# Products on half of the array in a two-layer network: one half after the other, or alternating

## The chip, the core and the metric

The program runs on one NeuronCore of a Trainium2 chip. The metric is the device time of one execution in microseconds (us). One execution was also recorded by the hardware profiler; all rows below come from that one. TensorE (PE) multiplies a stationary operand, which a weight load (PEld) puts into its array of 128 rows by 128 columns, with a moving operand, and writes into PSUM banks. VectorE (DVE), ScalarE (ACT) and GpSimd (POOL) do the rest; SyncE (SP) issues the DMAs.

## The reference, cut to what matters

A sequence of 512 positions with 1024 channels passes an even layer, an odd layer and a hybrid layer. Each has feed-forward parts, which take most of the time and which the change leaves alone. The mixers hold what the change touches, all of it in f32:

- Even layer, S5 branch: 32 groups of 16 channels, each with 64 complex states. The output of a group is what its own inputs give within blocks of eight positions, plus the real and the imaginary part of the state at the block's start, each times a matrix.
- Even layer, SSD branch (Mamba-2): eight heads of 64 channels in four pairs. A head's output is a masked product inside each chunk (`y_diag`) plus a product with the state carried in (`y_off`).
- Odd layer: attention with eight heads of 64 channels. `scores = q k^T / 8 + bias`, a softmax over the causal band, and the product with `v`.
- Hybrid layer: three attentions, plain and dilated, with eight heads of 64 channels each, combined by their softmax denominators; beside them a convolution of 31 taps and gates.

## The kernel before

Channels lie on the 128 partitions, so two heads of 64 channels, or the states of two S5 groups, lie in one tile: the first in partitions 0 to 63, the second in 64 to 127. A product over the 64 channels of one head uses only one half of the array's rows; a product whose result has 64 channels uses one half of its columns. The program's own operations go through small helpers, so all matmuls show as line L294 and all transposes as L297; the operands' names tell them apart. The large projections hold f32 values as a sum of two rounded parts (`xh` and `xl`, `wh` and `wl`) and make three products; the small products named here are plain f32 matmuls, which the trace shows as two instructions each.

A scheduler orders the instructions of each engine by priorities and a simulated clock. Where the code is inside `self.pe_order()`, TensorE's instructions keep the order in which the code emits them; work from outside such a region may still come between.

**S5** (`even`, the loop over `gh` and `gq`). Each quarter `gq` loads `tq` (cleared by POOL, then eight DMAs) and `cq` (two DMAs) into the tag `par`, which has three buffers. For each of its eight groups `g` it makes three products into one accumulator: `tq` with `ug` (all 128 rows), then `cq` with `hr` and `cq` with `hi` (64 rows, half `g2`). The two halves write into two banks, `pv[0]` and `pv[1]`. These products are not in a fixed order.

**SSD** (`ssd`, `out_y` and `out_o`), inside a fixed order: for head `s` of the pair all chunks `c`, then for the other head. The results of the two heads lie in different partitions of one bank, so each uses one half of the array's columns.

**Odd attention** (`odd`), inside a fixed order. There are 32 units, one for each pair of heads `j`, head `s` and block `qt` of 128 queries, in that order. `score` makes one product of 64 rows with N = 128 (qt + 1) keys (`qk` tiles, `qn` in the trace) into a bank `aux`; VectorE adds the bias `bt` and takes the maximum, ScalarE makes the exponentials `p`. `turn` transposes `p` on TensorE and copies it out (`pT`), `values` multiplies with `vt`. The loop over units is a pipeline written by hand:

```python
turn(u)
if n:
    values(units[n - 1])
...
if n + 2 < 32:
    score(units[n + 2])
for _ in range(share[j][n % 8]):
    next(plan[j], None)
```

so a unit's score stands two units ahead of its transposes, and `plan` fills in steps of the next pair's projections and other work. The bias `bt` of a head is loaded by SP when the head's first score is emitted (two buffers), and POOL then overwrites a corner of it.

**Hybrid attention** (`hybrid` and the class `AttnState`), with the same pipeline: 32 units of pair `j`, `kind` (plain, or the two dilated ones), head `s` and half `up` of the sequence. A score makes two products (plain) or four (dilated) from the tiles `r`. `filler` puts in projections and, for each of its steps, convolution taps on VectorE; from unit 22 on the projections of its first list are used up, and a new list starts at unit 26.

There are eight PSUM banks: three `mm`, three `aux`, two `acc`.

Of the kernel before, what the change touches and what calls it, by code (L numbers as in the profile page):

```python
# [17 lines left out]
T = 512  # L18
# [233 lines left out]
class Net:  # L252
# [721 lines left out]
    def even(self, gain):  # L974
# [110 lines left out]
        for gh in range(2):  # L1085
            pv = [self.psum("aux").rearrange("p (g c) -> p g c", g=8) for _ in range(2)]
            for gq in (2 * gh, 2 * gh + 1):
                tq = q.tile([128, 8, 128], F32, name="par", tag="par", bufs=3)

                nc.gpsimd.memset(tq, 0.0)  # L1090
                for s in range(8):
                    nc.sync.dma_start(tq[16 * s:16 * s + 16, :, 16 * s:128], self.d_kt[:, 8 * gq:8 * gq + 8, 0:128 - 16 * s])
                cq = q.tile([128, 2, 4, 128], F32, name="par", tag="par", bufs=3)
                for ri in range(2):
                    nc.sync.dma_start(cq[:, ri], self.d_cp[ri, :, 4 * gq:4 * gq + 4])
                for g in range(8):
                    j, g2 = g // 2, g % 2
                    s = slice(64 * g2, 64 * g2 + 64)
                    o = pv[g2][:, 4 * (gq % 2) + j]
                    self.mm(o, tq[:, g], ug[:, 8 * gq + g], True, False)  # L1100
                    self.mm(o, cq[s, 0, j], hr[s, 4 * gq + j], False, False)
                    self.mm(o, cq[s, 1, j], hi[s, 4 * gq + j], False, True)
            ysb = q.tile([128, 16, 64], F32, name="ysb", tag="ysb", bufs=1)
            for g2 in range(2):
                self.act(ysb[:, g2:16:2], pv[g2], AF.Copy)
            for t in range(8):
                nc.sync.dma_start(dy[256 * gh:256 * gh + 256, t].rearrange("(g i) c -> i g c", i=16), ysb[16 * t:16 * t + 16])
# [180 lines left out]
    def ssd(self, q, xs, bc, ya):  # L1288
# [50 lines left out]
        def out_y(j):  # L1339
            psY = psYs[j] = self.psum("acc")  # L1340
            xdt, mts = xdts[j], mtss[j]
            for s in range(2):
                hs = slice(64 * s, 64 * s + 64)
                for c in range(4):
                    self.mm(psY[hs, C(c)], xdt[:, 128 * c + 64 * s:128 * c + 64 * s + 64], mts[s][:, C(c)], True, True)

        def out_o(j):
            g = j // 2
            psO, psY = self.psum("acc"), psYs[j]
            hst, ea = hsts[j], eas[j]  # L1350
            for s in range(2):
                hs = slice(64 * s, 64 * s + 64)
                for c in range(1, 4):
                    o = 128 * (c - 1) + 64 * s
                    self.mm(psO[hs, C(c)], hst[:, o:o + 64], bc[:, 2 + g, C(c)], True, True)
            y = ya[j]
            self.stt(y, xs[:, j], self.vec("ssd_d", j), psY, ALU.mult, ALU.add)
            self.mul(ea[:, 128:], ea[:, 128:], psO[:, 128:])
            self.add(y[:, 128:], y[:, 128:], ea[:, 128:], self.on("ea") if j < 3 else None)
# [4 lines left out]
    def odd(self, gain):  # L1364
# [101 lines left out]
        Wo = self.stream(A["od_out"][0], 4)  # L1466
        fill = out0(Wo)

        def score(u):
            j, s, qt = u["j"], u["s"], u["qt"]  # L1470
            q = qa
            qk = args[j][0]
            if qt == 0:
                bt = q.tile([128, T], F32, name="bt", tag="bt", bufs=2)
                nc.sync.dma_start(bt, A["relb"][2 * j + s])
                nc.gpsimd.memset(bt[0:64, 448:512], NEG)
                self.bt = bt
                if s == 0:
                    args[j].append(q.tile([128, 4, 2], F32, name="st", tag="st", bufs=2))
            hs = slice(64 * s, 64 * s + 64)  # L1480
            N = 128 * (qt + 1)
            ps = self.psum("aux")
            self.mm(ps[:, 0:N], qk[0][hs, C(qt)], qk[1][hs, 0:N], True, True)
            p = u["p"] = q.tile([128, T], F32, name="p", tag="p", bufs=3)
            m = q.tile([128, 2], F32, name="m", tag="m", bufs=4)
            nc.vector.tensor_tensor_reduce(out=p[:, 0:N], in0=ps[:, 0:N], in1=self.bt[:, T - N:], scale=1.0, scalar=NEG,
                                           op0=ALU.add, op1=ALU.max, accum_out=m[:, 0:1])
            self.ts(m[:, 1:2], m[:, 0:1], -1.0, None, ALU.mult)
            self.act(p[:, 0:N], p[:, 0:N], AF.Exp, bias=m[:, 1:2], accum_out=args[j][2][:, qt, s:s + 1])

        def turn(u):
            qt = u["qt"]
# [43 lines left out]
        OP = ['0000010001202', '00000001111020020020', '0011000002000200002', '001010010003003000133']  # L1536
        for _ in mix(*[((pr[0], po[0], po[1])[int(c)], 1) for c in OP[0]], (pr[0], ALL), (po[0], ALL)):
            pass
        units = [dict(j=j, s=s, qt=qt) for j in range(4) for s in range(2) for qt in range(4)]
        plan = [mix(*[((pr[n + 1], po[n + 1], po[n + 2] if n < 2 else None, fill)[int(c)], 1) for c in OP[n + 1]],  # L1540
                    (pr[n + 1], ALL), (po[n + 1], ALL)) for n in range(3)] + [fill]
        share = [[1, 2, 3, 1, 3, 0, 1, 9], [2, 2, 2, 2, 3, 0, 1, 9], [2, 2, 2, 3, 1, 3, 1, 9], [1, 1, 1, 0, 0, 1, 0, 0]]
        next(plan[0])
        score(units[0])
        score(units[1])
        next(plan[0])
        for n, u in enumerate(units):
            j = u["j"]
            turn(u)
            if n:  # L1550
                values(units[n - 1])
            if n % 8 == 2 and n > 8:
                finish(j - 1)
            if n + 2 < 32:
                score(units[n + 2])
            for _ in range(share[j][n % 8]):
                next(plan[j], None)
        values(units[31])
# [15 lines left out]
    def hybrid(self):  # L1574
# [87 lines left out]
        order = self.pe_order()  # L1662
        order.__enter__()
        at8 = AttnState(self, q, rots, vts, oo, oT)
        units = [dict(j=j, kind=kind, s=s, up=up) for j in range(4) for kind in range(2) for s in range(2) for up in range(2)]

        def early():
            for s in HY_STEPS[:HY_STEPS.index("g0")]:
# [20 lines left out]

        filler(LEAD)  # L1690

        at8.score(units[0])
        at8.score(units[1])
        for n, u in enumerate(units):
            if n == SW:
                filler(99)
                for _ in taps:
                    pass
                side.close()
                gp = side.enter_context(tc.tile_pool(name="hyg", bufs=1, side="right", reuse_waits="tile"))  # L1700
                fill = late()
            k = SHARE[n]
            at8.turn(u)
            filler(k // 2)
            at8.values(u)
            if n % 8 == 2 and n > 8:
                at8.finish(u["j"] - 1)
            if n + 2 < 32:
                at8.score(units[n + 2])
            filler(k - k // 2)  # L1710
        for _ in fill:
            pass
# [335 lines left out]
class AttnState:  # L2048
# [5 lines left out]
        self.net, self.nc, self.q, self.rots, self.vts, self.oo = net, net.nc, q, rots, vts, oo  # L2054
        self.st, self.ps, self.oT = {}, {}, oT

    def score(self, u):
        net, nc, q = self.net, self.nc, self.q
        j, kind, s, up = u["j"], u["kind"], u["s"], u["up"]
        C = lambda c: slice(128 * c, 128 * c + 128)  # L2060
        if s == 0 and up == 0:
            self.st[j, kind] = q.tile([128, 4, 2, 2], F32, name=f"st{kind}", tag=f"st{kind}", bufs=2)
        st = self.st[j, kind]
        mask = net.cst("mask12" if kind else "mask0")
        hs = slice(64 * s, 64 * s + 64)
        ps = net.psum("aux")
        p = u["p"] = q.tile([128, T], F32, name="p", tag="p", bufs=3)
        ng = q.tile([128, 2], F32, name="ng", tag="ng", bufs=4)
        lo = u["lo"] = [0, 0]
        for uu in range(2):  # L2070
            t = 2 * up + uu
            b = 256 * uu
            if kind == 0:
                r = self.rots[j, 0]
                lo[uu] = 128 if t == 0 else 0
                k0 = 128 * (t - 1) + lo[uu]
                net.mm(ps[:, b + lo[uu]:b + 256], r[hs, 0, C(t)], r[hs, 1, k0:128 * t + 128], True, True)
            else:
                for i in range(2):
                    r = self.rots[j, 1 + i]  # L2080
                    net.mm(ps[:, b + 128 * i:b + 128 * i + 128], r[hs, 0, C(t)], r[hs, 1, C(t)], True, True)
        for uu in range(2):
            t = 2 * up + uu
            sl = slice(256 * uu + lo[uu], 256 * uu + 256)
            nc.vector.tensor_tensor_reduce(
                out=p[:, sl], in0=ps[:, sl], in1=mask[:, lo[uu]:256],
                scale=1.0, scalar=NEG, op0=ALU.add, op1=ALU.max, accum_out=st[:, t, s, 0:1])
        net.ts(ng, st[:, 2 * up:2 * up + 2, s, 0], -1.0, None, ALU.mult, eng=net.on("ng"))
        for uu in range(2):
            t = 2 * up + uu  # L2090
            sl = slice(256 * uu + lo[uu], 256 * uu + 256)
            net.act(p[:, sl], p[:, sl], AF.Exp, bias=ng[:, uu:uu + 1], accum_out=st[:, t, s, 1:2])

    def turn(self, u):
        net, nc = self.net, self.nc
# [90 lines left out]
```

## Time and profile before

| what | value |
|---|---|
| median of 3 runs | 2797.98 us (2795.88 to 2798.4) |
| the profiled execution's own time | 2793.72 us |
| its span, first to last instruction | 2791.9 us |
| mean granted TensorE clock | 0.981 |
| TensorE busy | 2718.7 us (97%) |
| VectorE, ScalarE, GpSimd busy | 67%, 57%, 32% |

TensorE's busy time is no measure of how fast it works: matmuls are pipelined, and the ends drawn are modelled, so an instruction can be drawn past the start of the next. The distance from one start to the next is what an instruction costs. [...]

### The profile page before, as it was taken

What the parts mean: (1) busy time and instruction counts of PE and PEld (TensorE: products, weight loads), DVE (VectorE), ACT (ScalarE), POOL (GpSimd) and SP (SyncE); (2) the same over time, 40 slices, a digit from 0 to 9 for tenths busy, and PEclk for the clock granted to TensorE, in tenths of its full rate; (3) what the DMA queues carried; (4) which work ended last, traced back from release to release, by engine and by line L of the source; (5) the groups of instructions that cost most, each with busy time, mean ns of one, the idle gap of its engine ahead of it and who ended that gap; (6) DMA issues with size and microseconds to landing.
All of it is one profiled execution on the core that took longest, in us unless ns stands there. A gap on an engine that the chain in (4) does not pass through costs nothing. (4 is left out here: it accounts for less than half of the span.)

```text
span 2791.9 us, 43952 instructions
## 1 busy us (share of the span) xinstructions
PE 2718.7 (97%) x16616; PEld 2410.2 (86%) x16616; DVE 1862.9 (67%) x3368; ACT 1581.1 (57%) x2525; POOL 893.8 (32%) x793
## 2 busy tenths in 40 slices
PE   8899999998999999999999999999999999999997
PEld 6798987878999999998777899988888788989997
DVE  7786756577576885866556758675786534666664
ACT  5366743646576776766334657663443443466674
POOL 5752513224344353342001433421000101345252
PEclk9999998999999999999999999999999899999998
DMA  5433346222332323324221233234333223233321
GB/s 181 120 105 106 95 159 128 82 71 69 103 114 99 106 87 108 113 92 127 69 72 63 67 109 108 98 114 143 92 90 94 68 90 107 69 91 105 115 88 57
DMA packets 106180, 277.44 MB, mean 99 GB/s; under 512 B 31920, under 2 KB 34608, under 8 KB 105968
## 3 DMA queue, kind: packets, MB, share of 16 engines
q1 hardware_dynamic: 105824, 274.44, 31.3%
q8 instruction: 131, 2.15, 0.3%
q14 instruction: 81, 0.66, 0.1%
q10 hardware_dynamic: 144, 0.18, 0.0%
HBM read 256.44 MB, written 11.85 MB: 96 GB/s over the span
## 5 line engine op out<-in xcount | busy, mean ns | idle before, releaser
L291 ACT ACTIVATE wh<-raw 128x1024 fp32r<-128x1024 f32 (+2 forms) x467 | 443.5, 954 | 610.8 <-PE mm L294 448.3
L294 PE MATMUL mm<-xh,wh 128*128 128x512 f32 (+1 forms) x1272 | 470.2, 370 | 9.5 <-ACT wh L291 7.1
L294 PE MATMUL mm<-xh,wl 128*128 128x512 f32 (+1 forms) x1272 | 459.8, 361 | 3.9 <-DVE wl L266 3.9
L294 PE MATMUL mm<-xl,wh 128*128 128x512 f32 (+1 forms) x1272 | 459.8, 361 | 2.4 <-DVE xl L281 2.4
L266 DVE TENSOR_TENSOR wl<-raw,wcopy 128x512 fp32r<-128x512 f32 (+1 forms) x408 | 255.7, 659 | 221.9 <-PE mm L294 92.6
L266 POOL TENSOR_TENSOR sa<-raw 128x512 f32<-128x512 f32 x92 | 120.8, 1313 | 610.7 <-DVE wl L266 307.8
L294 PE MATMUL mm<-th,wh 128*128 128x256 f32 x1104 | 309.6, 280 | 2.8 <-ACT wh L291 2.8
L294 PE MATMUL mm<-tl,wh 128*128 128x256 f32 x1104 | 308.1, 279 | 0.0
L294 PE MATMUL mm<-th,wl 128*128 128x256 f32 x1104 | 308.0, 279 | 0.0
L266 DVE TENSOR_TENSOR wl<-raw,wh 128x1024 fp32r<-128x1024 f32 (+1 forms) x171 | 222.7, 1303 | 124.5 <-ACT wh L291 119.1
L294 PEld LDWEIGHTS mm<-xh,wh 128*128 128x128 f32 x1272 | 244.4, 192 | 53.2 <-issue 8.7
L294 PEld LDWEIGHTS mm<-xh,wl 128*128 128x128 f32 x1272 | 244.2, 192 | 41.9 <-DVE wl L266 5.3
L294 PEld LDWEIGHTS mm<-xl,wh 128*128 128x128 f32 x1272 | 244.2, 192 | 36.8 <-DVE xl L281 4.9
L294 PE MATMUL aux<-xh,wl 128*128 128x256 f32 (+1 forms) x896 | 269.7, 301 | 2.2 <-DVE wl L266 2.2
L294 PE MATMUL aux<-xh,wh 128*128 128x256 f32 (+1 forms) x896 | 270.2, 302 | 1.6 <-ACT wh L291 1.2
L294 PE MATMUL aux<-xl,wh 128*128 128x256 f32 (+1 forms) x896 | 269.0, 300 | 0.0
L291 ACT ACTIVATE wcopy<-raw 128x512 fp32r<-128x512 f32 (+1 forms) x408 | 227.8, 573 | 9.0 <-DVE wl L266 8.1
L294 PEld LDWEIGHTS mm<-th,wh 128*128 128x128 f32 x1104 | 207.8, 188 | 3.0 <-ACT wh L291 3.0
L294 PEld LDWEIGHTS mm<-th,wl 128*128 128x128 f32 x1104 | 207.4, 188 | 0.0
L294 PEld LDWEIGHTS mm<-tl,wh 128*128 128x128 f32 x1104 | 207.2, 188 | 0.0
L294 PEld LDWEIGHTS aux<-xh,wh 128*128 128x128 f32 x896 | 172.8, 193 | 7.8 <-ACT wh L291 1.6
L294 PEld LDWEIGHTS aux<-xh,wl 128*128 128x128 f32 x896 | 172.2, 192 | 8.1 <-DVE wl L266 2.6
(485 smaller groups left out, 6723.3 us busy)
## 6 DMA issues: line engine op xcount, KB each, us to landing
raw<-in_gu SPq DMA_DIRECT2D x220, 512.0 KB, 3.8
raw<-in_wd SPq DMA_DIRECT2D x80, 448.0 KB, 3.3
raw<-in_hy_in SPq DMA_DIRECT2D x60, 512.0 KB, 3.8
raw<-in_wd SPq DMA_DIRECT2D x40, 512.0 KB, 3.5
raw<-in_ev_in SPq DMA_DIRECT2D x17, 512.0 KB, 3.8
raw<-in_od_in SPq DMA_DIRECT2D x16, 512.0 KB, 3.8
sw<-qk SPq DMA_DIRECT2D x48, 128.0 KB, 2.3
raw<-in_ev_out SPq DMA_DIRECT2D x8, 512.0 KB, 3.9
```

The source lines that it names most:

```text
L266: return (eng or self.nc.vector).tensor_tensor(out=out, in0=a, in1=b, op=op)
L291: return self.nc.scalar.activation(out, a, func, **kw)
L294: self.nc.tensor.matmul(ps, a, b, start=start, stop=stop)
```

## The change

In four places, products on the one and on the other half of the array, which stood in two runs, are emitted in turns. For the S5 products this comes with a fixed order on TensorE in each quarter. For the scores the units are reordered so that the two heads of a pair follow each other, and one call of `score`, at every even unit, makes both; the two biases `bt` are loaded together, with three buffers in place of two; the filler steps in `share` are distributed a little differently in the odd block (sums of the first seven 11, 12, 14 before; 11, 12, 13 after). All products and their operands stay what they were.

```diff
-                for g in range(8):
-                    j, g2 = g // 2, g % 2
-                    s = slice(64 * g2, 64 * g2 + 64)
-                    o = pv[g2][:, 4 * (gq % 2) + j]
-                    self.mm(o, tq[:, g], ug[:, 8 * gq + g], True, False)
-                    self.mm(o, cq[s, 0, j], hr[s, 4 * gq + j], False, False)
-                    self.mm(o, cq[s, 1, j], hi[s, 4 * gq + j], False, True)
+                with self.pe_order():
+                    for j in range(4):
+                        o = [pv[g2][:, 4 * (gq % 2) + j] for g2 in range(2)]
+                        for g2 in range(2):
+                            self.mm(o[g2], tq[:, 2 * j + g2], ug[:, 8 * gq + 2 * j + g2], True, False)
+                        for ri, h in enumerate((hr, hi)):
+                            for g2 in range(2):
+                                s = slice(64 * g2, 64 * g2 + 64)
+                                self.mm(o[g2], cq[s, ri, j], h[s, 4 * gq + j], False, ri == 1)
...
         def out_y(j):
-            for s in range(2):
-                hs = slice(64 * s, 64 * s + 64)
-                for c in range(4):
+            for c in range(4):
+                for s in range(2):
+                    hs = slice(64 * s, 64 * s + 64)
                     self.mm(psY[hs, C(c)], xdt[:, 128 * c + 64 * s:128 * c + 64 * s + 64], mts[s][:, C(c)], True, True)
         def out_o(j):
-            for s in range(2):
-                hs = slice(64 * s, 64 * s + 64)
-                for c in range(1, 4):
+            for c in range(1, 4):
+                for s in range(2):
+                    hs = slice(64 * s, 64 * s + 64)
...
-        def score(u):
-            j, s, qt = u["j"], u["s"], u["qt"]
+        def score(us):
+            j, qt = us[0]["j"], us[0]["qt"]
...
+                for s in range(2):
+                    bt = q.tile([128, T], F32, name="bt", tag="bt", bufs=3)
+                    nc.sync.dma_start(bt, A["relb"][2 * j + s])
+                    nc.gpsimd.memset(bt[0:64, 448:512], NEG)
+                    self.bt.append(bt)
...
+            pss = [self.psum("aux") for _ in us]
+            for u, ps in zip(us, pss):
+                hs = slice(64 * u["s"], 64 * u["s"] + 64)
+                self.mm(ps[:, 0:N], qk[0][hs, C(qt)], qk[1][hs, 0:N], True, True)
+            for u, ps in zip(us, pss):
...
-        units = [dict(j=j, s=s, qt=qt) for j in range(4) for s in range(2) for qt in range(4)]
+        units = [dict(j=j, s=s, qt=qt) for j in range(4) for qt in range(4) for s in range(2)]
-        share = [[1, 2, 3, 1, 3, 0, 1, 9], [2, 2, 2, 2, 3, 0, 1, 9], [2, 2, 2, 3, 1, 3, 1, 9], [1, 1, 1, 0, 0, 1, 0, 0]]
+        share = [[2, 2, 2, 1, 2, 1, 1, 9], [2, 2, 2, 2, 2, 1, 1, 9], [2, 2, 2, 2, 2, 1, 2, 9], [1, 1, 1, 0, 0, 1, 0, 0]]
...
-            if n + 2 < 32:
-                score(units[n + 2])
+            if n % 2 == 0 and n + 2 < 32:
+                score(units[n + 2:n + 4])
```

In `hybrid` the units and the call of `at8.score` change in the same way (`up` before `s`), and `AttnState.score` makes the products of both heads in turns:

```diff
-        units = [dict(j=j, kind=kind, s=s, up=up) for j in range(4) for kind in range(2) for s in range(2) for up in range(2)]
+        units = [dict(j=j, kind=kind, s=s, up=up) for j in range(4) for kind in range(2) for up in range(2) for s in range(2)]
...
+            for i in range(1 + kind):
+                for u, ps in zip(us, pss):
+                    hs = slice(64 * u["s"], 64 * u["s"] + 64)
+                    r = self.rots[j, i + kind]
+                    if kind == 0:
+                        k0 = 128 * (t - 1) + lo[uu]
+                        net.mm(ps[:, b + lo[uu]:b + 256], r[hs, 0, C(t)], r[hs, 1, k0:128 * t + 128], True, True)
+                    else:
+                        net.mm(ps[:, b + 128 * i:b + 128 * i + 128], r[hs, 0, C(t)], r[hs, 1, C(t)], True, True)
```

After the products, the maxima, the negations (`ng`) and the exponentials of the first head are emitted, then those of the second.

## Rows read from the trace of the kernel before

**Rows 1.** Windows, four stretches: time, busy us (instructions) by engine, clock, DMA.
```profile
core 0: us, PE busy (x) PEld busy (x) DVE busy (x) ACT busy (x) POOL busy (x), PEclk, DMA share, GB/s
448.10:500.80 52.70, 52.31 (x255) 43.27 (x253) 30.38 (x37) 20.16 (x27) 17.95 (x15) 0.77 0.36 99
1340.00:1505.00 165.00, 164.75 (x839) 128.68 (x838) 92.12 (x239) 65.22 (x131) 1.22 (x9) 0.99 0.21 65
1920.00:2190.00 270.00, 268.67 (x1365) 222.96 (x1364) 200.20 (x331) 110.32 (x207) 14.85 (x26) 1.00 0.33 96
2192.20:2222.00 29.80, 25.47 (x99) 19.63 (x97) 18.67 (x53) 14.12 (x35) 5.09 (x7) 0.60 0.14 37
```

**Rows 2.** Timeline of TensorE, S5 products: start, us, instruction.
```profile
455.62 0.45 PE L294 MATMUL aux<-hr,par 64*128 64x64 f32 x4
...
494.34 0.44 PE L294 MATMUL aux<-hr,par 64*128 64x64 f32 x4
494.61 0.39 PE L294 MATMUL aux<-hi,par 64*128 64x64 f32 x4
494.93 0.43 PE L294 MATMUL aux<-ug,par 128*128 128x64 f32 x2
495.30 0.43 PE L294 MATMUL aux<-hr,par 64*128 64x64 f32 x2
495.57 0.38 PE L294 MATMUL aux<-hi,par 64*128 64x64 f32 x2
495.88 0.43 PE L294 MATMUL aux<-ug,par 128*128 128x64 f32 x2
```

**Rows 3.** Timeline of TensorE, odd attention: a score and what follows it.
```profile
1429.13 0.48 PE L294 MATMUL aux<-qn 64*128 64x128 f32 x2
1429.54 0.50 PE L294 MATMUL mm<-xh,wh 128*128 128x512 f32 x1
```

**Rows 4.** Groups by shape, the scores: count, busy us, mean ns, idle before.
```profile
L294 PE MATMUL aux<-r 64*128 64x128 f32 x144 | 22.7, 291 | 0.0
...
L294 PE MATMUL aux<-r 64*128 64x256 f32 x48 | 15.9, 447 | 0.0
...
L294 PE MATMUL aux<-qn 64*128 64x512 f32 x16 | 9.0, 641 | 0.0
...
L294 PE MATMUL aux<-qn 64*128 64x384 f32 x16 | 7.3, 535 | 0.0
...
L294 PE MATMUL aux<-qn 64*128 64x256 f32 x16 | 5.9, 452 | 0.0
...
L294 PE MATMUL aux<-qn 64*128 64x128 f32 x16 | 3.9, 322 | 0.0
```

**Rows 5.** Timeline of TensorE, SSD products of the first pair of heads.
```profile
546.09 1.25 PE L294 MATMUL acc<-mt,xdt 128*64 128x128 f32 x13
...
547.24 0.27 PE L294 MATMUL acc<-bc,hst 128*64 128x128 f32 x1
547.29 0.27 PE L294 MATMUL acc<-mt,xdt 128*64 128x128 f32 x1
...
548.26 0.38 PE L294 MATMUL aux<-xde,btok 128*128 128x128 f32 x1
```

**Rows 6.** Timeline of TensorE, hybrid attention, with idle time before and its releaser.
```profile
2179.80 1.16 PE L294 MATMUL aux<-r 64*128 64x128 f32 x8
2180.89 0.50 PE L294 MATMUL mm<-xh,wh 128*128 128x512 f32 x1
...
2197.52 1.19 PE L297 MATMUL aux<-csts,p 128*128 128x128 f32 x4 [0.99 <-ACT p L291]
2199.39 1.97 PE L294 MATMUL acc<-vt,pT 128*128 128x64 f32 x8 [0.69 <-ACT pT L291]
```

**Rows 7.** Windows, two stretches of the hybrid attention; columns as in rows 1.
```profile
1940.00:1960.00 20.00, 20.00 (x101) 16.55 (x100) 19.27 (x28) 6.81 (x12) 0.21 (x1) 1.00 0.38 104
1940.00:2120.00 180.00, 179.84 (x909) 149.16 (x908) 152.14 (x252) 73.77 (x135) 8.80 (x15) 1.00 0.32 93
```

**Rows 8.** Instructions on the tile `bt`, last line: its eight loads.
```profile
DMA to landing us min/median/max: 2.6/3.4/5.3
```

More of the change, by code (lines that the diff above doesn't have):

```diff
@@ L1467, in odd @@
         fill = out0(Wo)
-        def score(u):
-            j, s, qt = u["j"], u["s"], u["qt"]
+        def score(us):
             q = qa
+            j, qt = us[0]["j"], us[0]["qt"]
             qk = args[j][0]
             if qt == 0:
[L1474 to L1480, printed above, removed]
-            N = 128 * (qt + 1)
[L1482 to L1489, printed above, removed]
@@ new lines, in score @@
+                self.bt = []
+                for s in range(2):
[3 more added lines that the diff above has]
+                    self.bt.append(bt)
+                args[j].append(q.tile([128, 4, 2], F32, name="st", tag="st", bufs=2))
+            N = 128 * (qt + 1)
+            pss = [self.psum("aux") for _ in us]
+            for u, ps in zip(us, pss):
+                hs = slice(64 * u["s"], 64 * u["s"] + 64)
+                self.mm(ps[:, 0:N], qk[0][hs, C(qt)], qk[1][hs, 0:N], True, True)
@@ new lines, in score @@
+            for u, ps in zip(us, pss):
+                s = u["s"]
+                p = u["p"] = q.tile([128, T], F32, name="p", tag="p", bufs=3)
+                m = q.tile([128, 2], F32, name="m", tag="m", bufs=4)
+                nc.vector.tensor_tensor_reduce(out=p[:, 0:N], in0=ps[:, 0:N], in1=self.bt[s][:, T - N:], scale=1.0,
+                                               scalar=NEG, op0=ALU.add, op1=ALU.max, accum_out=m[:, 0:1])
+                self.ts(m[:, 1:2], m[:, 0:1], -1.0, None, ALU.mult)
+                self.act(p[:, 0:N], p[:, 0:N], AF.Exp, bias=m[:, 1:2], accum_out=args[j][2][:, qt, s:s + 1])
@@ L1538, in odd @@
             pass
-        units = [dict(j=j, s=s, qt=qt) for j in range(4) for s in range(2) for qt in range(4)]
+        units = [dict(j=j, s=s, qt=qt) for j in range(4) for qt in range(4) for s in range(2)]
         plan = [mix(*[((pr[n + 1], po[n + 1], po[n + 2] if n < 2 else None, fill)[int(c)], 1) for c in OP[n + 1]],
                     (pr[n + 1], ALL), (po[n + 1], ALL)) for n in range(3)] + [fill]
-        share = [[1, 2, 3, 1, 3, 0, 1, 9], [2, 2, 2, 2, 3, 0, 1, 9], [2, 2, 2, 3, 1, 3, 1, 9], [1, 1, 1, 0, 0, 1, 0, 0]]
+        share = [[2, 2, 2, 1, 2, 1, 1, 9], [2, 2, 2, 2, 2, 1, 1, 9], [2, 2, 2, 2, 2, 1, 2, 9], [1, 1, 1, 0, 0, 1, 0, 0]]
         next(plan[0])
-        score(units[0])
-        score(units[1])
+        score(units[0:2])
         next(plan[0])
@@ L1690, in hybrid @@
         filler(LEAD)
-        at8.score(units[0])
-        at8.score(units[1])
+        at8.score(units[0:2])
         for n, u in enumerate(units):
@@ L1707, in hybrid @@
                 at8.finish(u["j"] - 1)
-            if n + 2 < 32:
-                at8.score(units[n + 2])
+            if n % 2 == 0 and n + 2 < 32:
+                at8.score(units[n + 2:n + 4])
             filler(k - k // 2)
@@ L2055, in __init__, with score @@
         self.st, self.ps, self.oT = {}, {}, oT
-    def score(self, u):
+    def score(self, us):
         net, nc, q = self.net, self.nc, self.q
-        j, kind, s, up = u["j"], u["kind"], u["s"], u["up"]
+        j, kind, up = us[0]["j"], us[0]["kind"], us[0]["up"]
         C = lambda c: slice(128 * c, 128 * c + 128)
-        if s == 0 and up == 0:
+        if up == 0:
             self.st[j, kind] = q.tile([128, 4, 2, 2], F32, name=f"st{kind}", tag=f"st{kind}", bufs=2)
@@ L2064, in score @@
         mask = net.cst("mask12" if kind else "mask0")
[L2065 to L2069, printed above, removed]
+        lo = [128 if kind == 0 and up == 0 else 0, 0]
+        pss = [net.psum("aux") for _ in us]
         for uu in range(2):
@@ L2072, in score @@
             b = 256 * uu
[L2073 to L2092, printed above, removed]
+            for i in range(1 + kind):
[7 more added lines that the diff above has]
+                        net.mm(ps[:, b + 128 * i:b + 128 * i + 128], r[hs, 0, C(t)], r[hs, 1, C(t)], True, True)
@@ new lines, in score @@
+        for u, ps in zip(us, pss):
+            s = u["s"]
+            u["lo"] = lo
+            p = u["p"] = q.tile([128, T], F32, name="p", tag="p", bufs=3)
+            ng = q.tile([128, 2], F32, name="ng", tag="ng", bufs=4)
+            for uu in range(2):
+                t = 2 * up + uu
+                sl = slice(256 * uu + lo[uu], 256 * uu + 256)
+                nc.vector.tensor_tensor_reduce(
+                    out=p[:, sl], in0=ps[:, sl], in1=mask[:, lo[uu]:256],
+                    scale=1.0, scalar=NEG, op0=ALU.add, op1=ALU.max, accum_out=st[:, t, s, 0:1])
+            net.ts(ng, st[:, 2 * up:2 * up + 2, s, 0], -1.0, None, ALU.mult, eng=net.on("ng"))
+            for uu in range(2):
+                t = 2 * up + uu
+                sl = slice(256 * uu + lo[uu], 256 * uu + 256)
+                net.act(p[:, sl], p[:, sl], AF.Exp, bias=ng[:, uu:uu + 1], accum_out=st[:, t, s, 1:2])
```

## Prediction

> **What bounds the kernel now.** I read first the busy time of each engine in the four stretches that hold the edited products [rows 1]. TensorE is the busiest in each: 52.31 of 52.7 us around the S5 products, 164.75 of 165 in the odd block's attention, 268.67 of 270 in the hybrid attention, but only 25.47 of 29.8 in a piece of the hybrid stage from 2192 us on. So in three of the four a microsecond taken off TensorE can move everything behind it. VectorE is next: 200.2 of 270 in the hybrid stage, and in the part from 1940 to 2120 us about 85% [rows 7]. The granted clock is 0.77 around S5 and 0.60 in the piece from 2192 us, about full speed elsewhere [rows 1].
>
> Second, the timeline of TensorE inside the S5 products [rows 2], which holds both orders side by side. A plain f32 matmul shows as two instructions (two passes). Where `hr` of one half of the array stands alone (x2), the next group starts 0.27 us later (495.30 to 495.57). Where the scheduler happened to put `hr` of both halves together (x4), the next starts 0.27 us later too (494.34 to 494.61); `hi` x4 takes 0.32, `hi` x2 0.31. So two products on different halves of the rows, written to different banks, take the time of one. That is what the argument rests on.
>
> Third, the edited groups by shape [rows 4], with the step from one start to the next [rows 3]; then the SSD products [rows 5], where `acc<-mt,xdt` of one column half and `acc<-bc,hst` of the other already overlap by accident at a boundary.
>
> **S5 state products.** Per group of 16 channels: `ug` 0.37, `hr` 0.27, `hi` 0.31, together 0.95 us (494.93 to 495.88 [rows 2]), so 1.90 for a pair. Afterwards a pair is `ug`, `ug`, `hr` x4, `hi` x4. The first `ug` keeps 0.37, `hr` x4 0.27 and `hi` x4 0.32. The second `ug` in a row is not shown here: it costs between nothing (fully beside the first) and 0.37 (as the first); both use the whole array, so I take 0.27, what two passes cost where the mode does not change (`hr` to `hi`). That makes 1.23, 0.67 less. There are 16 pairs; four already have `hr` and `hi` together (the first at 455.62 us, the last at 494.34 [rows 2]). 12 x 0.67 = 8.0 us at full clock. The stretch runs at 0.77 [rows 1], so the same work takes 1/0.77 as long: **10.4 us** (bounds with the second `ug` at 0.37 and at 0: 8.9 and 14.6).
>
> The fixed order adds a possible wait: a pair's `hr` now stands behind both `ug`, and behind a late `cq` load every later product of that quarter waits. Its `par` slot comes free only when products of the quarter before are read, and a load then needs some 3.4 us to land (the median of the bias loads [rows 8], taken as an estimate for these). Projections, which the scheduler may still put between, cover it today: TensorE idles 0.39 us in the whole stretch [rows 1]. A quarter gets 4 x 0.67 = 2.7 us shorter, so in each of three gaps 0 to 2.7 us can lie bare, 0 to 8 in all. Today's 0.39 is near the low end; with less work as cover I charge 2.4. S5 gives **8**.
>
> **SSD products.** Eight `out_y` and six `out_o` products are 28 instructions, from 546.09 to 548.26 us: 2.17 us [rows 5]. Where two column halves alternate, a start follows every 0.05 to 0.06 us (547.24, 547.29). 28 x 0.055 = 1.54, plus about 0.2 to leave the mode (the same 0.2 as for the scores, below) is 1.74: 0.43 less, four times: 1.7 us. No row here shows TensorE as the bound of that stage, so I take **1** (bounds 0 and 1.7).
>
> **Scores of the odd block.** The four shapes are busy 9.0 + 7.3 + 5.9 + 3.9 = 26.1 us in 32 products [rows 4]. The modelled end runs past the next start: a 64x128 pair of passes is drawn 0.48 us long and the next instruction starts after 0.41 [rows 3], so 32 x 0.07 = 2.2 comes off: 23.9 us, the way out of the mode included. The way in costs 0.10 more (`ug` to `hr` 0.37 against `hr` to `hi` 0.27 [rows 2]), 32 times: 3.2. Of 27.1 us half goes when two heads run side by side and share one way in and out: **13.5 us**. The bounds: long streams don't overlap (only 16 ways in and out saved: 16 x 0.3 = 4.8; see the rivals) and 13.5.
>
> What this edit moves costs nothing, by the following cover. The even-numbered unit's score stays where it was; the odd one's moves one unit earlier, so its softmax gets more time. Three `aux` banks suffice: each new tile takes the bank of a tile read at least one unit before. Three `p` buffers are just enough: the second takes the one that `turn` has just read. The bias `bt` is loaded for both heads at once: two DMAs and two memsets where there was one each. With three buffers the second head's load waits until the first head's last softmax of the pair before; it is issued on SP, ahead of weight blocks, lands after 3.4 us, 5.3 at most [rows 8], and the unit that needs it turns nine or more filler steps later. Uncovered it would cost 5.3 us in three of the four pairs. `share` keeps the same sum of filler steps but for one; order of fillers costs nothing.
>
> **Scores of the hybrid mixer.** 22.7 + 15.9 = 38.6 us in 32 units [rows 4]; 2.2 off as before, 3.2 added: 39.6. Half is **19.8 us**. The order of units again only brings the second head forward. From 2192 us on there is no filler left, so TensorE waits there for softmax and copies, 0.99 us for `p`, 0.69 for `pT` among others [rows 6]. That stretch's first `p` wait should go, because that unit's score is now issued a unit earlier; the copies' waits stay. Against that VectorE will sometimes be late: 20 us of a stage of 300 hold 20/300 of the saving, 1.3 us, and the fullest 20 us leave VectorE 0.73 idle [rows 7]. Over the nine such windows up to 2120 us, 28 us of idle time stand against 12 of saving, so most of it fits; I charge 2: **18** (bounds: 20 less those 12, and 20 with 3 of waits saved).
>
> **Sum.** 8 + 1 + 13.5 + 18 = 40.5, taken as 40 us. The profiled execution took 2793.72 us, its span 2791.9; it lies 4.3 us under the median of the runs, 2797.98. So a span of about 2752 and a median of **2758 us**. A change under 0.2% (5.6 us) can't be told from none.
>
> **The rivals.**
> *VectorE and the loads hold part of it* (2770 to 2788). If the saving between 1940 and 2120 us is lost, 10 us more go than I charge; with the `cq` load uncovered 6 more: 24 left, 2774. For it: the fullest window [rows 7]. Against: over the whole stage VectorE has 70 us idle [rows 1]. [...]
>
> *Only short products overlap* (about 2778). The x4 rows show 64 columns; the scores have 128 to 512. If long streams ran one after the other, the scores would save just the shared ways in and out, 16 x 0.3 in each attention, with S5 and SSD some 19 us. Against: passes of 128 columns on one half take 1.09/8 = 0.14 us each [rows 6], way in and out included, while on two column halves alternately one starts every 0.055 [rows 5].
>
> *The clock dips around S5 go as well* (about 2745). [...] For it: they lie in the stretch of the S5 products, which gets shorter. Against: no row shows which of its work brings them.
>
> *The clock falls in the attentions* (slower than before). The granted clock is 0.99 and 1.00 there [rows 1], and fell to the lower level where waits and short products without projections between stood together, from 2192 us on. [...] Against: the projections stay, and with them a TensorE without idle time. [...]
>
> *The order does nothing*, because the scheduler reorders: excluded, as scores and SSD products stand inside a fixed TensorE order before as after.
>
> **How the numbers follow.** Forecast 0.70 (its own range 2748 to 2769); held back in part 0.13; long streams not overlapping 0.05; dips gone too 0.07; the clock falling 0.05. Faster by over 0.2%: 0.70 + 0.13 + 0.05 + 0.07, less 0.02 for a held-back case that loses nearly all: 0.93. Within: those 0.02 and 0.01 of the falling clock. Slower: 0.04. The range 2741 to 2782 leaves out the slower cases, the worst of the held-back ones and the best of the dips.
>
> **What would show it.** `aux<-qn` x4 of 64x512 with the next start about 1.05 us behind (9.0/8 less 0.07, as now for x2); `aux<-r` x16 in 1.1 us; S5 pairs about 1.2 us apart at full clock; SSD's 28 instructions in 1.75 us; the odd stage about 13 us shorter, the hybrid 18, S5 8. Wrong if pairs start one after the other, if TensorE sits idle over 5 us behind `p`, `bt` or `par`, or if the attentions' clock falls under 0.95.

## The result and the profile after

The changed kernel takes 2754.78 us (median of 4 runs, 2747.58 to 2762.91), the kernel before, beside it, 2798.19 (2795.88 to 2800.06): a ratio of 0.9847, 95% interval 0.9835 to 0.986. The forecast was 2758. The profiled execution is the longest of the four, 2762.91 us with a span of 2761.0 at a granted clock of 0.981. That is a mean, as a share of full speed: in the traces of before and after the granted clock is at each moment either 1.00 or 0.50, called the low clock here (before, 0.50 from 2197 to 2220 us and 1.00 from 2180 to 2196).

The scores first. The groups by shape, over the whole span (count, busy us, mean ns, idle before), answer to [rows 4]:
```profile
L294 PE MATMUL aux<-r 64*128 64x128 f32 x144 | 11.3, 289 | 0.0
...
L294 PE MATMUL aux<-r 64*128 64x256 f32 x48 | 7.9, 439 | 0.0
...
L294 PE MATMUL aux<-qn 64*128 64x512 f32 x16 | 4.5, 641 | 0.0
...
L294 PE MATMUL aux<-qn 64*128 64x384 f32 x16 | 3.7, 535 | 0.0
...
L294 PE MATMUL aux<-qn 64*128 64x256 f32 x16 | 2.8, 428 | 0.0
...
L294 PE MATMUL aux<-qn 64*128 64x128 f32 x16 | 2.0, 322 | 0.0
```
Counts and mean lengths are those of before but for at most 24 ns; the busy time, in which overlapping instructions count once, is half in each row, the longest streams (512 columns) included. The timeline of TensorE shows it for one call of two heads in the odd block, and one in the hybrid mixer (start, us, instruction), as [rows 3] and the first lines of [rows 6] did for one head:
```profile
1374.65 1.13 PE L294 MATMUL aux<-qn 64*128 64x512 f32 x4
1375.71 0.50 PE L294 MATMUL mm<-xh,wh 128*128 128x512 f32 x1
...
2158.27 1.16 PE L294 MATMUL aux<-r 64*128 64x128 f32 x16
2159.36 0.50 PE L294 MATMUL mm<-xh,wh 128*128 128x512 f32 x1
```
The next instruction starts 1.06 and 1.09 us behind; the forecast said 1.05 and 1.1. One head alone took 1.09 for x8 [rows 6], so the second one adds less than 0.01 us.

The S5 products, answering to [rows 2]: a pair at full clock (1.00), and the one long wait of the stretch, whose releaser stands in brackets:
```profile
465.06 0.66 PE L294 MATMUL aux<-ug,par 128*128 128x64 f32 x4
465.65 0.44 PE L294 MATMUL aux<-hr,par 64*128 64x64 f32 x4
465.92 0.39 PE L294 MATMUL aux<-hi,par 64*128 64x64 f32 x4
466.24 0.66 PE L294 MATMUL aux<-ug,par 128*128 128x64 f32 x4
...
483.37 0.69 PE L294 MATMUL aux<-hr,par 64*128 64x64 f32 x4 [3.12 <-DMA par<-d_cp]
```
A pair takes 1.18 us (465.06 to 466.24): both `ug` 0.59, `hr` 0.27, `hi` 0.32. The second `ug` costs 0.22 over the 0.37 of the first. The wait at 483.37 is the late `cq` load.

The SSD products [rows 5] are now two groups, 16 and 12 instructions, from 555.90 to 557.58: 1.68 us where it was 2.17.
```profile
555.90 1.09 PE L294 MATMUL acc<-mt,xdt 128*64 128x128 f32 x16
556.82 0.82 PE L294 MATMUL acc<-bc,hst 128*64 128x128 f32 x12
557.58 0.49 PE L294 MATMUL aux<-xde,btok 128*128 128x128 f32 x2
```

To see where the time went, I cut both traces at the same projections of TensorE, so that each window holds the same work: 605 instructions around S5, 1274 around the odd attention, 1919 around the hybrid stage. The windows of before (length, busy us of each engine, then clock), and those of after:
```profile
core 0: us, PE busy (x) PEld busy (x) DVE busy (x) ACT busy (x) POOL busy (x), PEclk, DMA share, GB/s
409.60:522.10 112.50, 108.04 (x605) 88.91 (x605) 62.72 (x79) 47.39 (x65) 30.43 (x26) 0.86 0.52 120
1320.90:1580.70 259.80, 252.19 (x1274) 201.27 (x1273) 151.93 (x326) 113.15 (x201) 28.61 (x31) 0.99 0.22 69
1907.00:2300.70 393.70, 387.78 (x1919) 320.27 (x1918) 254.58 (x442) 168.82 (x309) 22.39 (x38) 0.97 0.31 92
```
```profile
415.60:516.60 101.00, 93.33 (x605) 78.31 (x605) 63.24 (x79) 46.20 (x64) 31.21 (x26) 0.90 0.59 133
1316.90:1565.10 248.20, 239.54 (x1274) 197.06 (x1273) 150.60 (x326) 111.09 (x201) 28.66 (x31) 0.98 0.23 72
1891.40:2270.60 379.20, 367.69 (x1919) 305.22 (x1918) 255.75 (x442) 161.90 (x305) 21.32 (x38) 0.98 0.32 95
```
11.5, 11.6 and 14.5 us went, 37.6 together; the profiled execution is only 30.8 us shorter. The difference of 6.8 was lost outside these windows, nearly all of it before the first edit: the same projection that comes at 134.9 us in the trace of before comes 6.0 us later here. A second profile of the same kernel (below) has it 2.5 us later, and 42 us saved in all.

What the readers of the scores do, answering to [rows 7] and [rows 8]: VectorE is busy 138.55 of 160 us in the first part of the hybrid stage, 87% where the trace of before has 83% from 1940 to 2100 us, and the eight loads of `bt` land a little sooner than they did.
```profile
1940.00:2100.00 160.00, 158.38 (x845) 131.95 (x844) 138.55 (x231) 69.55 (x131) 8.81 (x15) 1.00 0.32 94
```
```profile
DMA to landing us min/median/max: 2.6/2.8/4.8
```

### The profile page after: what moved, and what is told of

The parts are those of the page before. It is cut to its first block, busy times and chain, and to the rows that moved or that the text cites. A ratio compares the mean times of both kernels' runs of the same rounds, so it can differ in the third digit from the quotient of the medians.

```text
span 2761.0 us, 43938 instructions
## 1 busy us (share of the span) xinstructions
PE 2676.4 (97%) x16616; PEld 2384.2 (86%) x16616; DVE 1867.5 (68%) x3368; ACT 1571.4 (57%) x2521; POOL 891.9 (32%) x793
```

## The experiments

**Each part alone.** Four kernels are the kernel before with one part of the diff. The lines at the core of each:
S5:
```diff
-                for g in range(8):
...
+                with self.pe_order():
+                    for j in range(4):
...
+                        for ri, h in enumerate((hr, hi)):
+                            for g2 in range(2):
```


> Only the S5 products alternate (in a fixed order); SSD and both attentions as before. Side by side (my theory): 12 pairs at 0.72 us less, a little more through the lower clock, less some 3 us behind a late load: 8 to 11 us faster than before. Rival, the gain of this part is only that of clock dips moving about: within 3 us of before, and pairs as long as before.

SSD:
```diff
-            for s in range(2):
-                hs = slice(64 * s, 64 * s + 64)
-                for c in range(4):
+            for c in range(4):
+                for s in range(2):
+                    hs = slice(64 * s, 64 * s + 64)
```


> Only the SSD products alternate. My theory: 28 instructions take 1.67 us in place of 2.17, four times, so 2 us at the place itself, of which 0 to 2 reach the end. Rival, VectorE sets this stage: 0. Both are within what the runs can tell, the profile has to.

Odd block:
```diff
-            if n + 2 < 32:
-                score(units[n + 2])
+            if n % 2 == 0 and n + 2 < 32:
+                score(units[n + 2:n + 4])
```


> Only the odd block's scores are paired (with the new unit order, biases and filler shares). Side by side: 11 to 13.5 us faster. Rival, the pairing gains only the shared way in and out of half-array products: 5 us or less.

Hybrid:
```diff
-            if n + 2 < 32:
-                at8.score(units[n + 2])
+            if n % 2 == 0 and n + 2 < 32:
+                at8.score(units[n + 2:n + 4])
```


> Only the hybrid mixer's scores are paired. Side by side with little held back: 16 to 20 us faster. Rival, VectorE holds it where it is nearly full: 8 to 12. The four parts' gains should add to that of the whole change (43 us) within some 6 us; a sum well under it would mean that the parts help each other.

Measured, against 2796.52 us of the kernel before on the same chip:

| part | median us | ratio, 95% interval | us | predicted |
|---|---|---|---|---|
| S5 | 2785.53 | 0.9964, 0.9953 to 0.9976 | -11.0 | -8 |
| SSD | 2798.63 | 1.0004, 0.9994 to 1.0013 | +2.1, none | -1 |
| odd | 2784.40 | 0.9955, 0.994 to 0.997 | -12.1 | -13.5 |
| hybrid | 2779.37 | 0.9936, 0.9921 to 0.9951 | -17.2 | -18 |

They add up to 38.2 us; the whole change saves 43.4 by its own medians, 44.5 in the second measurement below. Each interval is 3 to 4 us wide to either side, so the parts add up within what they can tell. SSD gives nothing that these runs can tell from no change; its trace says more. TensorE's waits for `mt` from 540 to 700 us (total, times, longest), before and with this part alone:
```profile
PE acc L294 <- DVE mt L266: 1.4, 1, 1.4
```
```profile
PE acc L294 <- DVE mt L266: 2.3, 2, 1.9
```
At the same projections this trace gains 1.1 us on that of before from 520 to 580 us and gives 0.5 back where TensorE, coming sooner, waits for `mt` of VectorE: 0.6 us stay, and the second profile of the whole change shows the same steps. Behind that, from 604 us on, a stretch at the low clock (0.50) loses 2.8 us; the traces with S5 alone and the hybrid part alone have such a stretch (3.4 us) at the same projections with the SSD products as before, so it isn't shown to come from this edit.

**Both heads on the same half.** If what pays is streaming side by side, it must go when both read the same rows.
```diff
-                hs = slice(64 * u["s"], 64 * u["s"] + 64)
+                hs = slice(0, 64)
```


> The changed kernel, but in the odd block and in the hybrid mixer the scores of both heads read the first 64 rows of the array (head 1's scores are left out: head 0's are computed twice). Count of products, banks, readers and order stay. If the gain of the scores comes from two heads streaming on different halves of the array side by side, a call's products now follow each other and only the shared way in and out of the half-array mode stays: 16 x 0.3 = 4.8 us in each attention instead of 13.5 and 19.8 as forecast, so 8.8 + 15 = 24 us are lost, near 2779 us, and qn x4 of 64x512 takes about 1.9 us instead of 1.06, r x16 about 2 instead of 1.09. The rival, that the gain comes from fewer changes of mode and from scores issued earlier, expects no loss: 2755 us, and the same steps from start to start.


Measured: 2774.35 us, ratio 0.9914 (0.9895 to 0.9933), 19.6 us longer than the changed kernel's 2754.78. The steps are those of the first theory; the timeline of TensorE:
```profile
1410.06 1.98 PE L294 MATMUL aux<-qn 64*128 64x512 f32 x4
1411.97 0.44 PE L297 MATMUL mm<-csts,v 128*128 128x128 f32 x2
...
1947.59 2.05 PE L294 MATMUL aux<-r 64*128 64x128 f32 x16
1949.57 0.50 PE L294 MATMUL mm<-xh,wh 128*128 128x512 f32 x1
```
1.91 in place of 1.06, and 1.98 in place of 1.09. So the rival falls: order and earlier scores alone don't bring it. The windows with the same work say what is left without overlap:
```profile
1311.70:1566.10 254.40, 247.87 (x1273) 202.25 (x1272) 151.13 (x326) 111.33 (x200) 28.65 (x31) 0.98 0.22 70
1892.40:2281.00 388.60, 383.49 (x1919) 320.05 (x1918) 256.08 (x442) 162.27 (x305) 21.36 (x38) 0.97 0.31 93
```
5.4 and 5.1 us less than before, where the prediction had 4.8 in each attention, 0.3 for each call that shares one start and one end of its half-array products. In the trace of before, at 2179.80 us, these show as 0.213 us from the first pass to the second and 0.202 from the last to the next product, where the passes between follow each other every 0.112: 0.19 more together. So the sum has the right size; the windows don't give it exactly, as they also hold other waits and, in the odd block, 3.4 us more at the low clock than before. By starts alone, two calls of one head take 2 x 1.085 us and this one 1.978: 0.19 of the 0.3 that the prediction counts for a call. The rest is overlap. It is smaller than expected, 6.2 us for 8.8 in the odd block and 9.4 for 15 in the hybrid stage: there TensorE stands still for only 5.1 of 388.6 us here, but for 11.5 of 379.2 in the changed kernel, so part of what the overlap frees turns into waits.

**Head after head.** Both heads in one call on their own halves, but not in turns.
```diff
-        for uu in range(2):
...
-            for i in range(1 + kind):
-                for u, ps in zip(us, pss):
+        for u, ps in zip(us, pss):
...
+            for uu in range(2):
...
+                for i in range(1 + kind):
```


> The changed kernel, but in the hybrid mixer a score call emits all products of head 0 and then all of head 1, instead of in turns. If TensorE looked no further ahead than the next product, only the last product of head 0 and the first of head 1 could overlap, and a dilated call (r x16) would take about 1.8 us instead of 1.09; if it reaches over several passes, as in the SSD products of the kernel before, where the second half started beside the fifth of eight passes, about 1.6. 16 calls times 0.5 to 0.7, with less for the local calls with few products: 4 to 8 us longer than the changed kernel, 2759 to 2763. The rival, that the order within a call does nothing since the hardware reorders freely, expects 1.09 still and 2755.


Measured: 2758.02 us, ratio 0.9856 (0.9837 to 0.9875), against 0.9847 and 0.9849 for the changed kernel: about 2 us longer, which these intervals can't tell from none. The trace can. A dilated call, and a plain one of four passes a head, in the timeline of TensorE:
```profile
1940.08 1.71 PE L294 MATMUL aux<-r 64*128 64x128 f32 x16
1941.72 0.50 PE L294 MATMUL mm<-xh,wh 128*128 128x512 f32 x1
...
2005.88 1.14 PE L294 MATMUL aux<-r 64*128 64x256 f32 x8
2006.95 0.50 PE L294 MATMUL mm<-xh,wh 128*128 128x512 f32 x1
```
1.64 us in place of 1.09, as expected for a second head that starts several passes early (about 1.6), and 1.07 for the plain call, as in turns (1.06). Eight dilated calls times 0.55 are 4.4 us, and the window with the same work holds as much: TensorE is busy 371.52 us, where the two profiles of the changed kernel have 367.69 and 367.09.
```profile
1886.50:2267.10 380.60, 371.52 (x1920) 309.49 (x1919) 254.57 (x442) 162.57 (x305) 22.44 (x38) 0.98 0.32 95
```
So the rival falls: the order within a call mattered here with eight passes in a row on one half (1.64 for 1.09), and not with four (1.07 for 1.06).

**S5 without its fixed order.**
```diff
-                with self.pe_order():
-                    for j in range(4):
+                for j in range(4):
```


> The changed kernel, but the S5 products without their fixed TensorE order, so that the scheduler may put them and projections between as it likes; the emission in turns stays. My theory: the pairs are what saves, and the fixed order costs one wait of 3.1 us for the cq load that the trace of the changed kernel shows at 480 us; the scheduler might fill that wait, or might split pairs again. 2752 to 2758 us if most pairs stay together. The rival, that without the fixed order the scheduler puts hr of the two halves apart as it did in the kernel before, expects most of the S5 gain gone: 2762 to 2766.


Measured: 2755.49 us, ratio 0.9849 (0.9832 to 0.9866): the same. 13 of the 16 pairs stay together (`hr` x4 and `hi` x4), so the rival falls; the wait for `cq` is gone from the waits of TensorE in this stretch, and single `ug` are split off from their pairs instead. The fixed order neither gains nor costs what can be measured.

**Filling the hole.** In the hybrid stage the first filler still runs out, as it did before [rows 6]. The stretch without filler in the changed kernel, in a window and in the timeline:
```profile
2169.50:2195.00 25.50, 19.25 (x98) 15.20 (x97) 18.34 (x41) 13.97 (x32) 5.47 (x7) 0.73 0.18 55
```
```profile
2176.61 1.05 PE L294 MATMUL mm<-ones,cs 128*128 128x1 f32 x8 [0.55 <-POOL cs L266]
2179.70 1.18 PE L297 MATMUL aux<-csts,p 128*128 128x128 f32 x3 [2.04 <-ACT p L291]
2181.53 1.54 PE L294 MATMUL acc<-vt,pT 128*128 128x64 f32 x6 [0.65 <-DVE pT L2114]
```
```diff
-TAPS = 2
-SHARE = [4, 4, 3, 3, 3, 3, 3, 4, 3, 3, 4, 3, 4, 4, 3, 4, 4, 4, 3, 3, 2, 3, 2, 3, 2, 3, 3, 3, 3, 3, 3, 3]
-SW = 26
+TAPS = 3
+SHARE = [4, 4, 3, 3, 3, 3, 3, 4, 3, 3, 4, 3, 4, 4, 3, 4, 4, 4, 3, 3, 2, 3, 2, 2, 2, 2, 2, 2, 2, 2, 2, 2]
+SW = 22
```


> The changed kernel with the second kind of filler work of the hybrid stage (gates and the output of the convolution) begun at unit 22, where the first kind runs out, instead of 26, with two steps a unit, and three taps of the convolution a step instead of two, so that its normalization is through by then. In the changed kernel TensorE has no filler from 2169.5 to 2195 us: 19.25 of 25.5 us busy at a granted clock of 0.73. If that stretch is filled, the idle 6.3 us and most of what the low clock costs there (13.7 us at half the rate, 6.9 us) go: 5 to 12 us shorter than the changed kernel, 2743 to 2750. The rival, that the taps set the time (VectorE is busy 46.6 of 50 us from 2050 to 2100 us and gets three taps a step now), expects waits on VectorE earlier in the stage that take it back: 2753 us or longer.


Measured: 2757.44 us, ratio 0.9852 (0.9832 to 0.9872): no gain, as the rival said. The place is filled (TensorE busy 48.4 of 50 us from 2150 to 2200), but a new wait stands earlier, for GpSimd and not for VectorE as the rival had it, and the granted clock, 0.90 from 2100 to 2150 us, fell there:
```profile
2115.62 1.87 PE L294 MATMUL mm<-ones,cs 128*128 128x1 f32 x8 [6.80 <-POOL cs L266]
```
A milder form begins the second filler at unit 24 and keeps two taps:
```diff
-SHARE = [4, 4, 3, 3, 3, 3, 3, 4, 3, 3, 4, 3, 4, 4, 3, 4, 4, 4, 3, 3, 2, 3, 2, 3, 2, 3, 3, 3, 3, 3, 3, 3]
-SW = 26
+SHARE = [4, 4, 3, 3, 3, 3, 3, 4, 3, 3, 4, 3, 4, 4, 3, 4, 4, 4, 3, 3, 2, 3, 2, 3, 3, 3, 3, 3, 2, 2, 2, 2]
+SW = 24
```


> The changed kernel with the second kind of filler of the hybrid stage begun at unit 24 instead of 26, and still two taps of the convolution a step. Begun at 22 with three taps, the hole without filler was indeed closed, but TensorE stood 6.8 us for the sums of the convolution's normalization (POOL cs) and the clock fell there for 10.2 us. With two taps a step the normalization is nearly through at unit 24, so my theory expects that wait under 2 us and about half of the hole's 6.3 us of idle time and of its slow clock gone: 3 to 6 us shorter than the changed kernel run beside it, 2749 to 2752. The rival, that the stage is tied by the chain convolution, normalization, gates and not by the order of fillers, expects the wait to move again and the time to stay within 2 us of the changed kernel.


Measured: 2752.16 us, ratio 0.984 (0.9827 to 0.9853), beside 2753.65 for the changed kernel. 1.5 us can't be told from none. The wait has moved again, to the next step of the same normalization:
```profile
2171.91 1.12 PE L297 MATMUL mm<-csts,small 128*128 128x128 f32 x4 [5.36 <-DVE small L281]
```
The wait for `cs` did go under 2 us (0.6), but the time didn't follow. So the rival held as far as two attempts show: moving projections only moves where TensorE waits in the chain of the convolution's normalization. Shortening that chain itself was not tried.

**The changed kernel again.**


> The changed kernel once more, beside the one before and the variant with the late filler from unit 24 on the same chip. Expected: 2755 us within 2, a ratio to the kernel before of 0.985; and the stretches at the low clock outside the edited stages at other places than in its first profile, which would show that the 10.1 us that S5 saved there, and the 6 us lost before 135 us, include dips that wander from run to run. The rival, that the change itself places these dips, expects them at the same times again.


Measured: 2753.65 us (2751.5 to 2758.15, 5 runs) against 2798.11, ratio 0.9849 (0.9836 to 0.9862). Its windows with the same work:
```profile
412.10:511.70 99.60, 93.82 (x605) 77.99 (x604) 63.27 (x79) 46.10 (x64) 31.19 (x26) 0.90 0.58 135
1309.40:1556.50 247.10, 240.08 (x1273) 197.17 (x1272) 150.35 (x326) 111.00 (x200) 28.60 (x31) 0.98 0.22 73
1882.80:2259.90 377.10, 367.09 (x1919) 304.88 (x1918) 255.59 (x442) 161.91 (x305) 21.32 (x38) 0.98 0.32 96
```
12.9, 12.7 and 16.6 us: 42.2 together, and its own time is 41.8 under that of the profiled execution of before (2751.97 against 2793.72). Some stretches at the low clock (0.50) lie elsewhere than in the first profile: those at 582.1, 599.1 and 1370.6 us (3.4 us each) are gone, one at 1506.0 (3.4 us) is new. The window around S5 holds 20.5 us of low clock in both, in three stretches at other places, and the hole of the hybrid stage 13.7 us in both. So each theory holds for some of the dips.

## Why the prediction was right

**Side by side.** Its central claim, taken from one accidental neighbourhood of `hr` products, holds for all widths measured, from 64 columns (`hr` x4 0.27 us, as x2) to 512 (`qn` x4 1.06, x2 1.05 in the trace of before), and in both attentions. The experiment on one half shows it: without different halves 1.06 becomes 1.91. The rival that only short products overlap falls with it. Its price was about right all the same: with only the starts and ends shared the windows are 5.4 and 5.1 us shorter.

**Odd scores: 13.5 forecast.** 12.1 alone; by the windows 13.9 alone (245.9 us), 11.6 and 12.7 in the two profiles of the whole change. What the sum didn't have is the clock. It is 0.50 for 6.8 us of the window before, for 3.4 in the kernel with the odd part alone, for 10.2 in both profiles after. By that share each us there loses half a us, an estimate; the measured loss is a little less, as a group of S5 products took 1.66 us at 0.50 (484.49 to 486.15) and 0.95 at 1.00 in the trace of before, which is 0.43 lost of each us. Taken at one half, 12.2, 13.3 and 14.4 us are saved at equal clock: the term was right.

**Hybrid scores: 18 forecast.** 17.2 alone, 16.6 in the window of the second profile, by three terms that are each off. The work of TensorE fell by 17.3 us and not by 19.8: the durations in the sum held four calls at the low clock, 1.6 to 2.0 us from start to start where such a call takes 0.85 or 1.06 elsewhere. 3.4 us, taken at one half, came from the clock (23.9 us at 0.50 before, 17.1 after), which the sum left as it was. Busy time together fell by 20.7 us (387.78 to 367.09). Against that idle time rose from 5.9 to 10.0, 4.1 where 2 was charged for late readers. The waits of TensorE in this stage (total, times, longest), before and in the first profile after:
```profile
PE aux L297 <- ACT p L291: 2.2, 3, 1.0
PE acc L294 <- DVE pT L2105: 1.4, 2, 0.8
```
```profile
PE aux L297 <- ACT p L291: 4.1, 3, 2.0
PE acc L294 <- DVE pT L2114: 3.4, 4, 1.2
```
In the second profile they are 4.0 and 3.5 us. The forecast also said that the first `p` wait of the stretch without filler would go; instead one of 2.04 us stands there. Late readers held back these 4.1 us, and no more: VectorE, 87% busy from 1940 to 2100 us, did not become the bound.

**S5: 8 forecast.** 11.0 alone (6.7 to 13.1 by its interval). The pair costs 1.18, not 1.23, since the second `ug` takes 0.22 and not 0.27; the load of `cq` was bare for 3.1 us (2.8 in the second profile) where 2.4 were charged. These two nearly cancel. What was mis-sized is the clock: the sum divided the saving by 0.77 and left the dips as they were, but the window ran at 0.90 and not at 0.86. It holds 30.7 us at 0.50 before and 20.5 in both profiles after, so, taken at one half, 5.1 us less are lost there; the other 6.4 and 7.8 us are work less the wait. That is no chance of one run. All twelve traces, cut at the same two projections:

| S5 products | traces | window, us | of it at the low clock, us | at equal clock, us |
|---|---|---|---|---|
| as before | 4 | 112.5 to 115.1 | 30.7 to 37.5 | 95.6 to 97.1 |
| in turns | 8 | 97.3 to 104.1 | 17.1 to 27.3 | 88.6 to 91.5 |

By the means some 6.7 us are work less the wait and 6.2 the clock. So the rival that the dips go too, given 7 in 100, came true in part (in full it is worth 12 us, 0.23 of the 52.7 us at a clock of 0.77 [rows 1]); that the clock's share comes with the edit is shown, why it does was not tested.

**SSD: 1 forecast.** The 28 instructions of the first pair take 1.68 us, 0.49 less (0.43 was worked out). Four times that is 2 us. The trace shows 0.6 left before 600 us, as half of 1.1 is given back behind VectorE; the runs can't tell 0.6 from nothing. In the kernel with this part alone the clock is at 0.50 for 6.8 us from 602.8 us on, where it was at 1.00 before, which hides the 0.6 in that trace.

**Held back, clock, order.** Waits for `p` and `pT` in the hybrid stage came to 4.1 and 3.4 us, not over 5 for either, but 7.5 together; those for `par` 3.1; for `bt` none shows in the lists read. The clock of the attentions stayed at 0.98 (0.99 and 0.97 before), so the case on the other side did not happen. Against the parts alone the errors had both signs: 3 too little for S5, about 1 too much for each of the other three. That the median came within 4 us is owed in part to that, which is luck: of the 6 us or so that the clock gave around S5 the sum held only the 2.4 that dividing by 0.77 added.

## What to carry to other kernels

Products that contract over 64 rows cost about half here (1.06 us for 1.91, 1.09 for 1.98) when two of them, on different halves of the rows (and, in all cases of this kernel, in different banks), stood next to each other in TensorE's order; look in the trace for two that already do by accident, and read the price of the pair off there. Such a change paid here as far as TensorE was busy without waits: in the S5 and attention stretches most of it came through (in the hybrid stage 16.6 of 20.7 us), in the SSD stage about half of what was gained went into a wait. Where a hole remains, name the chain that ends last in it before moving other work in: after two attempts at it TensorE waited 6.8 and 5.4 us elsewhere in that chain, and nothing was won that could be measured.

## What was unexpected of the hardware

In a dilated call of the changed kernel (2136.55 us and on, single instructions of its trace) the passes of 128 columns on one half start 0.112 us apart from the second on, and in turns the other half's pass starts 0.007 us after its partner. With one head after the other (1940.08), the second head's first pass starts at 1940.635, right behind the fifth pass of the first head at 1940.629 and before its sixth at 1940.740. The records don't name the half; the first pass of each is told by its length, 0.373 us against 0.272 for the others. So in this trace the second head's products start ahead of three passes that stand before them in the program. The call's length says the same: 1.98 us with both heads on one half, less three times 0.112, is the 1.64 measured. It was three as well in the plain call, where the second head starts beside the first of four passes (2005.878 and 2005.891), and in the SSD products of the kernel before [rows 5], where the second half of the columns began at 546.584 beside the fifth of eight.
